# A decoder layer on eight cores: V tiles with a ones column, chained first loads, w_out sums on VectorE, and a merged last down projection

## The chip, the cores and the metric

The kernel runs on all 8 cores of one Trainium2 chip. Each core computes the whole layer for its own 1,152 tokens (1,024 of a prompt, 128 of samples), plus a small halo; the cores exchange nothing. The time is in device microseconds of the slowest core, lower is better.

In the profiled run of the kernel before, the clock record of cores 4 and 5 has 0.81 from 52 to 210 us, apart from shorter stretches at 0.50. So I read stage times from **quiet cores** (those whose clock was not lowered).

## The reference, cut to what matters

```python
h = rmsnorm(x); q, k, v, B, C, u = split(h @ w_in)
A = windowed attention(q, k, v)         # 16 heads, 4 KV heads, window 128, ALiBi, a sink logit in the denominator
S = B * dwconv3(C * u)                  # gated short convolution
x = x + concat(rmsnorm(A), rmsnorm(S)) @ w_out
h = rmsnorm(x)
x = x + (silu(dwconv3(h @ w_gate) + b) * (h @ w_up)) @ w_down     # d_model 2048, d_ff 5632
y = rmsnorm(x)
```

Softmax here needs two products with the same exponentials: their product with V, and their sum (the denominator).

## The kernel before

Activations lie feature-major: features on the 128 partitions, tokens along the free dimension. The stages are, in order: **stage one** (load x in three token tiles, and K, V, Q projections); **attention**, whose small matmuls are interleaved step by step with the dense B, C, u projections so that PE always has work; a **handover** that computes the two norm factors of the mixed halves; **w_out**; the **FFN** in 11 groups of gate, up and down; and the **end** (the last down projection, final norm, output). Matmuls are written through one helper (line L209 in the profile), most additions through another (L234), activations through L230, and so on; one profile line is therefore many places.

Stage one, the loads and the projections (cut):

```python
T.dma("sp", cf, cf_d)
xload(0)                                   # four DMAs, one per quarter of the features
wload(0)                                   # K weights; float32 in HBM, cast to bf16 by the DMA
T.dma("pool", cb, cb_d)
wload(1, after=[st0[0][:, 0, :]])          # "after": wait until that piece has landed
T.dma("sp", scT..., sct_d)
xload(1)
wload(2, after=[st0[0][:, 0, :]])
wload(3, after=[st0[0][:, 0, :]])
norm1(0)                                   # hT = x * g on VectorE, squares on ScalarE, their sums on VectorE
xload(2)
p = [k_task(0, 0), k_task(1, 0)]           # matmuls; the returned functions evict with the norm factor
rstd1(0, 7)                                # the norm factor, by a ones matmul and Ln/Exp
for f in p: f()
norm1(1)
for i in range(4): v_task(i)()
# ... tiles 1 and 2 in the same manner
```

Attention, the product with V (per block of 128 queries; `lt` holds exponentials, which are the stationary operand):

```python
oo = psb[b0 + half][:, g * 65:g * 65 + 64]
od = psb[b0 + half][:, g * 65 + 64:g * 65 + 65]
T.mm(oo, lt, vtm[:, vt, j * 64:(j + 1) * 64], start=(op == 0), stop=(op == 1), skip=True)
T.mm(od, lt, onesb[:, 0:1], start=False, stop=(op == 1), skip=True)       # the denominator: one column
```

The interleaving gives each dense step an equal share of the attention steps, though dense steps are 260, 384 or 512 columns wide:

```python
tgt = min(m, ((i + 1) * m + n - 3) // max(1, n - 2))
while si < tgt:
    step(pr, seq[si]); si += 1
```

Handover and w_out (48 steps, of 16 matmuls each: the attention half into pA, the convolution half into pB):

```python
rA_calc()
for ti in range(3): rB_calc(ti, 7)         # each with a reciprocal on VectorE
for oc in range(16):
    for ti, (a, b) in enumerate(FT):
        # 8 matmuls into pA, 8 into pB
        T.tt("dve", u1, pA[:, 0:W], rA[:, a:b], ALU.mult)
        T.tt("pool", x2, x2, u1, ALU.add)
        T.tt("dve", u2, pB[:, 0:W], accB[:, a:b], ALU.mult)
        T.tt("dve", x2, x2, u2, ALU.add)
        T.act(h2T[:, oc, a:b], x2, AF.Copy, scale=col(V_GF + oc))
        T.act(sq, x2, AF.Square)
        T.tt("pool", acc2[:, a:b], acc2[:, a:b], sq, ALU.add)
```

In the first gate/up step all three norm sums of the FFN (`r2_calc`) stand between the gate and the up matmuls. The end:

```python
LT = [(0, 512), (512, 1024), (1024, 1152)]
for ti, (a, b) in enumerate(LT):
    for oc in range(16):
        # 4 matmuls (group 10 alone)
        T.tt("dve", x3, ps[:, 0:W], x3, ALU.add)
        T.act(sq3[it % 2][:, 0:W], x3, AF.Square)
        T.tt("pool", acc3[:, a:b], acc3[:, a:b], sq3[it % 2][:, 0:W], ALU.add)
        # after oc 2: the norm of the tile before; then one output per step, scaled on VectorE
```

The softmax here doesn't subtract the row's maximum and nothing guards it: scores larger than these inputs give would overflow.

Of the kernel before, what the change touches and what calls it, by code (L numbers as in the profile page):

```python
# [8 lines left out]
ALU = mybir.AluOpType  # L9
# [294 lines left out]
FT = [(0, 385), (385, 770), (770, 1154)]  # L304
WINS = 18

def build_nc(same_engine_sync=True):
    nc = bass.Bass("TRN2", target_bir_lowering=False)  # L308
    with ExitStack() as es:
# [99 lines left out]
        vtm = V(o, [11, 256], BF16); o += 5632  # L409
# [3 lines left out]
        kf = V(o, [2, 256]); o += 2048  # L413
        vf = V(o, [2, 256]); o += 2048
# [20 lines left out]
        o = O_H2 + 36928  # L435
        rA = V(o, [NC]); o += 4616
# [42 lines left out]
        def xload(t):  # L479
            for q in range(4):  # L480
                T.dma("sp", st0[t][:, 4 * q:4 * q + 4, :], xt_d[t][:, 4 * q:4 * q + 4, :])
# [15 lines left out]
        def rstd1(t, bank):  # L497
            a, b = TX[t]
            W = b - a
            T.mm(psb[bank][:, 0:W], onesf, S4[t][:, 0, :])  # L500
            ln = S4[t][:, 1, :]
            T.act(ln, psb[bank][:, 0:W], AF.Ln, bias=epsc, scale=1.0 / D)
            T.act(r1[:, a:b], ln, AF.Exp, scale=-0.5)
            q0 = max(a, 126)
            T.act(r1q[:, q0 - 126:b - 126], ln[:, q0 - a:], AF.Exp, scale=-1.0)
            tl = [i for i, (c0, c1) in enumerate(VT) if a <= c0 < b]
            for i in tl:
                c0, c1 = VT[i]
                T.mm(psb[bank][0:c1 - c0, i:i + 1], r1[0:1, c0:c1], onesf[0:1, 0:1])
                T.copy("act", r1c[0:c1 - c0, i:i + 1], psb[bank][0:c1 - c0, i:i + 1])  # L510
# [4 lines left out]
        T.dma("pool", cb, cb_d)  # L515
        wload(1, after=[st0[0][:, 0, :]])
        T.dma("sp", scT.rearrange("p a b -> p (a b)"), sct_d)
        xload(1)
        wload(2, after=[st0[0][:, 0, :]])
        wload(3, after=[st0[0][:, 0, :]])  # L520
        norm1(0)
        xload(2)

        dbank = {"i": 0}

        def nb():
            b = dbank["i"] % 4
            dbank["i"] += 1
            return b
# [13 lines left out]
        def v_task(i):  # L543
            c0, c1 = VT[i]
            rows = c1 - c0
            ps = psb[nb()]
            for k in range(16):
                T.mm(ps[0:rows, 0:256], hT[:, k, c0:c1], wk(1, k, 0, 256), start=(k == 0), stop=(k == 15))

            def post():  # L550
                T.act(vtm[0:rows, i, :], ps[0:rows, 0:256], AF.Copy, scale=r1c[0:rows, i:i + 1])
                if i >= 9:
                    T.act(vf[:, i - 9, :], ps[:, 0:256], AF.Copy, scale=r1c[:, i:i + 1])
            return post
# [11 lines left out]

        p = [k_task(0, 0), k_task(1, 0)]
        rstd1(0, 7)
        for f in p:
            f()  # L570
        norm1(1)
        for i in range(4):
            v_task(i)()
        p = [q_task(0, 0, 2), q_task(1, 0, 2)]
        for f in p:
            f()
        k_p = [k_task(0, 1), k_task(1, 1)]
        rstd1(1, 6)
        for f in k_p:
            f()  # L580
        norm1(2)
        for i in range(4, 7):
            v_task(i)()
        for qc in range(2):
            q_task(qc, 1, 2)()
        for t in range(2):
            for qc in (2, 3):
                q_task(qc, t, 3)()
        k_p = [k_task(0, 2), k_task(1, 2)]
        wload(4)  # L590
        rstd1(2, 5)
        for f in k_p:
            f()
        T.dma("sp", kw_d, kf.rearrange("p a b -> p (a b)"))
        for i in range(7, 11):
            v_task(i)()
        wload(5)
# [6 lines left out]
        wload(7)  # L604

# [51 lines left out]
        def att_PV(pr, G, bl):  # L657
            n = 2 * G + bl + 1
            b0 = ab2()
            for g in range(4):  # L660
                for half in range(2):
                    j = 2 * pr + half
                    for op in range(2):
                        oo = psb[b0 + half][:, g * 65:g * 65 + 64]
                        od = psb[b0 + half][:, g * 65 + 64:g * 65 + 65]
                        lt = Ef_(half, g)[:, (op * 2 + bl) * 128:(op * 2 + bl + 1) * 128]
                        vt = n + 1 - op
                        T.mm(oo, lt, vtm[:, vt, j * 64:(j + 1) * 64], start=(op == 0), stop=(op == 1), skip=True)
                        T.mm(od, lt, onesb[:, 0:1], start=False, stop=(op == 1), skip=True)
# [40 lines left out]
        def halo_PV(pr):  # L710
            b0 = ab2()
            for g in range(4):
                for half in range(2):
                    j = 2 * pr + half
                    s = slice(half * 8 + g * 2, half * 8 + g * 2 + 2)
                    oo = psb[b0 + half][0:2, g * 65:g * 65 + 64]
                    od = psb[b0 + half][0:2, g * 65 + 64:g * 65 + 65]
                    T.mm(oo, EhO[:, s], vtm[:, 1, j * 64:(j + 1) * 64], start=True, stop=False, skip=True)
                    T.mm(od, EhO[:, s], onesb[:, 0:1], start=False, stop=False, skip=True)
                    T.mm(oo, EhP[0:2, s], vtm[0:2, 0, j * 64:(j + 1) * 64], start=False, stop=True, skip=True)  # L720
                    T.mm(od, EhP[0:2, s], onesb[0:2, 0:1], start=False, stop=True, skip=True)
# [49 lines left out]
        def samp_PV(pr):  # L771
            b0 = ab2()
            X, Y = psb[b0], psb[b0 + 1]
            for half in range(2):
# [4 lines left out]
                T.mm(X[pb:pb + 64, :], vtm[:, 10, j * 64:(j + 1) * 64], en, start=True, stop=False, skip=True)  # L779
# [89 lines left out]
        def att_seq(pr):  # L869
# [14 lines left out]
            out += [("SS", 0), ("SS", 1), None, ("SP",)]  # L884
# [30 lines left out]
        def run(pr, dense):  # L915
# [4 lines left out]
            for i, d in enumerate(dense):  # L920
# [9 lines left out]
                tgt = min(m, ((i + 1) * m + n - 3) // max(1, n - 2))  # L930
# [6 lines left out]
                late.clear()  # L937
            while si < m or early or late or trq:
# [41 lines left out]
        run(1, bdense(range(4, 8)))  # L980
        T.dma("sp", cvo_d, cuk.rearrange("p a b -> p (a b)"))

# [7 lines left out]
        def rB_calc(ti, bank):  # L990
            a, b = FT[ti]
# [3 lines left out]
            T.recip(ln[:, 0:W], r1q[:, a + 2:b + 2])  # L995
            T.ts("dve", ln, ln, EPS, None, ALU.mult)
            T.stt("dve", ln, psb[bank][:, 0:W], 1.0 / 1024, ln, ALU.mult, ALU.add)
            T.act(ln, ln, AF.Ln)
            T.act(accB[:, a:b], ln, AF.Exp, scale=-0.5)

        def rA_calc():
# [6 lines left out]
            b0 = 4  # L1008
            dg = Af[0]
            T.tt("dve", dg[0:2, 0:2], ident[0:2, 0:2], rAc[0:2, 0:1].to_broadcast([2, 2]), ALU.mult)  # L1010
            T.mm(psb[6][:, 0:2], onesf[0:2, :], dg[0:2, 0:2])
# [5 lines left out]
            dgs = [V(O_H2 + 8192 + 4752 + 2048 + 2176 + i * 512, [128]) for i in range(8)]  # L1017
            for n in range(1, 9):
                T.ts("dve", dgs[n - 1], ident, rAc[:, n:n + 1], None, ALU.mult)
# [5 lines left out]
        rA_calc()  # L1025
        for ti in range(3):
            rB_calc(ti, 7)

        it = 0
        for oc in range(16):  # L1030
            si = WINS + oc // 2
            T.dma("sp", x2T[:, oc, :], xr_d[oc])
            for ti, (a, b) in enumerate(FT):
                W = b - a
                pA, pB = psb[(2 * it) % 8], psb[(2 * it + 1) % 8]
                for k in range(8):
                    T.mm(pA[:, 0:W], wk(si, k, oc % 2), mixedT[:, k, a:b], start=(k == 0), stop=(k == 7))
                for k in range(8, 16):
                    T.mm(pB[:, 0:W], wk(si, k, oc % 2), mixedT[:, k, a:b], start=(k == 8), stop=(k == 15))
# [3 lines left out]
                T.tt("pool", x2, x2, u1, ALU.add)  # L1043
# [9 lines left out]
            if oc % 2 == 1:  # L1053
                wload(si + 4)
# [38 lines left out]
        calc = {"todo": True}  # L1093

        def gateup(grp):
            ab = actb[grp % 2]
            for hg in range(2):
# [3 lines left out]
                for ci in range(2):  # L1101
                    f = grp * 4 + hg * 2 + ci
                    fi = hg * 2 + ci
                    for ti, (a, b) in enumerate(FT):
# [7 lines left out]
                        if calc["todo"]:  # L1112
                            for t_ in range(3):
                                r2_calc(t_, 4 + t_)
                            calc["todo"] = False
# [52 lines left out]
        for grp in range(11):  # L1168
            gateup(grp)
            if grp >= 1:  # L1170
# [5 lines left out]
        ab = actb[0]  # L1176
        LT = [(0, 512), (512, 1024), (1024, 1152)]
        acc3 = V(O_H2, [1152])
        r3 = V(O_H2 + 4608, [1152])
        sq3 = [V(O_H2 + 9216 + i * 2048, [512]) for i in range(2)]  # L1180
        yst = V(O_H2 + 9216 + 4096, [4, 512])

        def fin_calc(ti):
            a, b = LT[ti]
            W = b - a
            bank = ti
            T.mm(psb[bank][:, 0:W], onesf, acc3[:, a:b])
            ln = sq3[0][:, 0:W]
# [3 lines left out]
        def fin_out(ti, oc):  # L1192
            a, b = LT[ti]
            x3 = x2T[:, oc, 2 + a:2 + b]
            T.stt("dve", x3, x3, col(V_GN + oc), r3[:, a:b], ALU.mult, ALU.mult)
            T.dma("sp", yt_d[oc, :, a:b], x3)

        pend = []
        it = 0
        for ti, (a, b) in enumerate(LT):  # L1200
            W = b - a
            for oc in range(16):
                ps = psb[4 + it % 4]
                for fi in range(4):
                    T.mm(ps[:, 0:W], dview(d0 + fi // 2)[:, fi % 2, oc * 128:(oc + 1) * 128], ab[:, fi, a:b],
                         start=(fi == 0), stop=(fi == 3))
                x3 = x2T[:, oc, 2 + a:2 + b]
                T.tt("dve", x3, ps[:, 0:W], x3, ALU.add)
                if oc == 0:
                    T.act(acc3[:, a:b], x3, AF.Square)  # L1210
                else:
                    T.act(sq3[it % 2][:, 0:W], x3, AF.Square)
                    T.tt("pool", acc3[:, a:b], acc3[:, a:b], sq3[it % 2][:, 0:W], ALU.add)
                it += 1
                if oc == 2 and ti > 0:
                    fin_calc(ti - 1)
                    pend += [(ti - 1, x) for x in range(16)]
                if pend:
                    fin_out(*pend.pop(0))
            
        for q in pend:
            fin_out(*q)
        fin_calc(2)
# [165 lines left out]
```

## Time and profile before

Three executions took 1704.71, 1738.67 and 1952.89 us. The profiled one took 1704.54. The list of cores of the kernel before (span and mean granted clock):

```profile
...
core 0: 1683.7 us, clock 0.974
...
core 4: 1702.6 us, clock 0.954
core 5: 1703.5 us, clock 0.954
...
core 7: 1685.1 us, clock 0.972
```

Six cores end at 1682 to 1685 us. Cores 4 and 5 had their clock lowered early and end about 20 us later.

Next the chain of waits, summed by engine, from the page of the slowest core (core 5):

```profile
...
PE 74%; POOL 7%; DVE 7%; issue 5%; ACT 4%; DMA 3%; SPq 0%; DVEq 0%; POOLq 0%; ACTq 0%
```

PE bounds most of it, but not all. Where the rest lies, the table by windows of quiet core 0 tells. I set the windows at the stage borders found in the trace: stage one, attention with the handover, w_out, the first gate matmul to the first up matmul, FFN, end. Columns are the window and its length, busy microseconds of each engine with the number of instructions, granted clock, mean share of busy DMA engines, and GB/s.

```profile
...
core 0: us, PE busy (x) PEld busy (x) DVE busy (x) ACT busy (x) POOL busy (x), PEclk, DMA share, GB/s
0.00:133.00 133.00, 86.33 (x493) 53.25 (x494) 49.76 (x84) 32.18 (x46) 4.76 (x12) 0.92 0.61 143
133.00:418.00 285.00, 272.91 (x2428) 166.93 (x2427) 159.69 (x399) 111.93 (x291) 60.96 (x81) 0.98 0.42 78
418.00:580.00 162.00, 133.03 (x770) 72.84 (x769) 70.24 (x137) 45.94 (x90) 79.71 (x91) 0.99 0.36 83
580.00:597.00 17.00, 7.77 (x22) 3.10 (x23) 5.90 (x12) 6.65 (x14) 9.42 (x12) 0.68 1.22 224
597.00:1571.00 974.00, 971.30 (x5938) 577.93 (x5937) 610.42 (x1177) 97.59 (x264) 148.78 (x196) 1.00 0.42 69
1571.00:1683.00 112.00, 74.22 (x391) 37.44 (x388) 83.18 (x146) 30.34 (x58) 47.76 (x47) 0.84 0.32 101
```

The FFN has PE busy for 971 of 974 us: nothing to gain there. Time without PE work lies in stage one (47 us), around the handover (12), in w_out (29), before the first up matmul (9) and in the end (38). The waits of PE on the same core (total, times, longest) name who was waited for:

```profile
...
PE psb L209 <- DVE arena L234: 49.9, 64, 3.6
PE psb L209 <- ACT arena L230: 20.7, 6, 8.8
PE psb L209 <- POOL arena L234: 18.8, 6, 7.0
PE psb L209 <- DMA arena<-win: 17.9, 1, 17.9
```

The 29.0 us of w_out are among the 49.9 us put down to VectorE. But one must ask what VectorE itself waited for, and the chain of waits, in order of time, tells it (start, duration, engine). These lines are one step of w_out on core 0, and the start of the next:

```profile
...
442.75 0.57 DVE arena L234
...
443.40 1.04 ACT arena L230 x2
...
444.51 1.83 POOL arena L234 x2
...
446.37 0.57 DVE arena L234
```

In each step, the two POOL additions take 1.83 us, ScalarE 1.04 and one VectorE addition 0.57, one after the other. The step takes 446.37 − 442.75 = 3.62 us, of which PE needs only 2.61 (16 matmuls that start 163 ns apart). POOL is in the loop, so it binds. The handover and the end show up in the same chain, as a reciprocal of 2.58 us (there are three) and as POOL additions without a break:

```profile
...
412.83 2.58 DVE arena L268
...
1614.35 1.28 POOL arena L234
...
1615.70 1.29 POOL arena L234
```

Last, two groups of the list by shape (busy time, mean ns of one | idle before): the products with V and with the ones column.

```profile
...
L209 PE MATMUL psb<-arena 128*128 128x64 bf16 x256 | 16.5, 190 | 2.1 <-DVE arena L234 2.0
L209 PE MATMUL psb<-arena 128*128 128x1 bf16 x256 | 16.0, 165 | 0.0
```

### The profile page before, as it was taken

To read this page: it belongs to the slowest core of one execution; us is meant where nothing else is said; L and a number is where in the kernel's file an instruction comes from. 1 tells how busy PE (TensorE), PEld (TensorE's weight loads), DVE (VectorE), ACT (ScalarE), POOL (GpSimd) and SP (SyncE) were. 2 spreads that over 40 slices of the span, in tenths; PEclk is the share of its full clock that TensorE was granted. 3 is DMA by queue.
4 is the path that set the end of the run, shared out by engine and by line. 5 is a ranking of instruction groups with operands and counts; after the bars stand their busy time and mean duration, and the time that the engine had idled before them with its cause. 6 is when DMAs were issued, how large, how long until landed. Compare 5 with 4: busy or idle time off the path is not lost.

```text
span 1703.5 us, 24149 instructions; the slowest of 8 cores (1681.7 to 1703.5 us)
## 1 busy us (share of the span) xinstructions
PE 1567.0 (92%) x10034; PEld 918.0 (54%) x10034; DVE 979.5 (58%) x1953; ACT 325.9 (19%) x761; POOL 351.4 (21%) x438
## 2 busy tenths in 40 slices
PE   2789999998887779999999999999999999999973
PEld 1555565655444345555555555555555556555531
DVE  3523563555543445575665757575656657575767
ACT  2312341444222221101001010101011010101042
POOL 0001121122255432111111010101111120101064
PEclk8778899999899989999999999999999999999985
DMA  9516236223922293533533534434435335335205
GB/s 197 169 31 118 50 51 99 50 51 67 256 43 45 44 171 60 87 62 53 92 54 62 87 50 74 75 50 76 73 50 82 68 50 94 55 61 88 44 34 189
DMA packets 26414, 136.98 MB, mean 80 GB/s; under 512 B 3072, under 2 KB 5376, under 8 KB 13952
## 3 DMA queue, kind: packets, MB, share of 16 engines
q0 software_dynamic: 13968, 98.92, 35.5%
q1 hardware_dynamic: 12336, 36.52, 7.2%
q8 instruction: 78, 1.28, 0.3%
q14 instruction: 32, 0.26, 0.1%
HBM read 223.47 MB, written 14.80 MB: 140 GB/s over the span
## 4 chain that ended last, share of the span: by engine, by line
PE 74%; POOL 7%; DVE 7%; issue 5%; ACT 4%; DMA 3%; SPq 0%; DVEq 0%; POOLq 0%; ACTq 0%
PE psb L209 74%; POOL arena L234 7%; ACT arena L230 4%; DVE arena L234 4%; DMA arena<-xt 3%; DVE arena L253 2%; DVE arena L246 0%; DVE arena L268 0%; PE psb L213 0%; POOL arena L204 0%; SPq L204 0%; ACT L230 0%; ACT arena L258 0%; DVE arena L260 0%; DVEq L169 0%
## 5 line engine op out<-in xcount | busy, mean ns | idle before, releaser
L209 PE MATMUL psb<-arena 128*128 128x384 bf16 (+8 forms) x9962 | 1564.4, 318 | 124.6 <-DVE arena L234 48.4
L209 PEld LDWEIGHTS psb<-arena 128*128 128x128 bf16 (+2 forms) x9962 | 912.9, 100 | 769.9 <-issue 66.8
L234 DVE TENSOR_TENSOR arena<-psb,arena 128x384 f32<-128x384 f32 (+10 forms) x1172 | 569.5, 504 | 506.3 <-POOL arena L234 226.2
L234 POOL TENSOR_TENSOR arena<-arena 128x385 f32<-128x385 f32 (+8 forms) x316 | 293.9, 935 | 873.4 <-ACT arena L230 795.9
L230 ACT ACTIVATE arena<-arena 128x385 f32<-128x385 f32 (+15 forms) x402 | 232.7, 601 | 1223.1 <-DVE arena L253 896.6
L253 DVE SCALAR_TENSOR_TENSOR arena<-arena 128x383 f32<-128x383 f32 (+3 forms) x360 | 231.2, 646 | 24.9 <-ACT arena L230 13.9
L234 DVE TENSOR_TENSOR arena<-arena 128x512 bf16<-128x512 bf16 (+9 forms) x149 | 82.6, 564 | 135.2 <-POOL arena L234 95.0
L246 DVE TENSOR_SCALAR arena<-arena 128x385 f32<-128x385 f32 (+9 forms) x215 | 88.6, 429 | 43.4 <-DMA arena<-xt 30.7
L230 ACT ACTIVATE arena<-psb,arena 128x256 bf16<-128x256 f32 (+5 forms) x167 | 64.6, 474 | 93.0 <-PE psb L209 92.8
L204 POOL DMA_DIRECT2D arena<-wu x22 | 12.4, 565 | 263.1 <-PE psb L209 263.1
L204 POOL DMA_DIRECT2D arena<-win x18 | 10.3, 574 | 169.3 <-PE psb L209 158.1
L258 ACT COPY arena<-arena 128x2 f32<-128x2 f32 (+1 forms) x140 | 23.8, 200 | 0.0
L258 ACT COPY arena<-psb 128x512 bf16<-128x512 bf16 (+5 forms) x31 | 12.0, 395 | 48.3 <-PE psb L213 43.7
L268 DVE RECIPROCAL arena<-arena 128x4 f32<-128x4 f32 (+3 forms) x39 | 14.0, 360 | 3.5 <-ACT arena L230 2.3
L204 POOL DMA_DIRECT2D arena<-wd x22 | 12.3, 562 | 0.2
L260 POOL COPY arena<-arena 128x2 f32<-128x2 f32 (+5 forms) x20 | 5.1, 269 | 32.7 <-DVE arena L234 31.6
L204 POOL DMA_DIRECT2D arena<-wg x22 | 11.8, 538 | 0.0
L213 PEld LDWEIGHTS psb<-arena 128*128 128x128 bf16 (+1 forms) x72 | 5.2, 99 | 3.5 <-issue 1.9
L213 PE MATMUL psb<-arena 128*128 128x128 bf16 (+1 forms) x72 | 6.5, 217 | 0.0
L253 DVE SCALAR_TENSOR_TENSOR arena<-psb,arena 128x8 f32<-128x8 f32 (+4 forms) x15 | 5.2, 374 | 0.7 <-PE psb L209 0.3
L204 POOL DMA_DIRECT2D arena<-wout x8 | 4.6, 574 | 0.3 <-issue 0.3
L230 ACT ACT_TABLE_LOAD x3 | 3.8, 1283 | 2.1 <-PEq L308 1.1
(11 smaller groups left out, 7.6 us busy)
## 6 DMA issues: line engine op xcount, KB each, us to landing
arena<-wg POOLq DMA_DIRECT2D x22, 1024.0 KB, 16.1
arena<-wu POOLq DMA_DIRECT2D x22, 1024.0 KB, 10.3
arena<-wd POOLq DMA_DIRECT2D x22, 1024.0 KB, 14.5
arena<-win POOLq DMA_DIRECT2D x18, 1024.0 KB, 10.8
arena<-xr SPq DMA_DIRECT2D x16, 577.0 KB, 21.8
arena<-wout POOLq DMA_DIRECT2D x8, 1024.0 KB, 10.0
yt<-arena SPq DMA_DIRECT2D x32, 256.0 KB, 2.1
arena<-xt SPq DMA_DIRECT2D x4, 1024.0 KB, 14.5
```

Source lines behind the costliest of these rows:

```text
L204: return self.add(q, lambda: eo.dma_start(out=out, in_=in_), [in_, *after], [out], dma=q)
L209: return self.add("pe", lambda: nc.tensor.matmul(out, lhsT, rhs, start=start, stop=stop, **kw), [lhsT, rhs], [out])
L213: return self.add("pe", lambda: nc.tensor.transpose(out, in_, ident), [in_, ident], [out])
L230: return self.add("act", lambda: nc.scalar.activation(out=out, in_=in_, func=func, **kw), rd, wr)
L234: return self.add(eng, lambda: eo.tensor_tensor(out=out, in0=in0, in1=in1, op=op), [in0, in1], [out])
L246: return self.add(eng, lambda: eo.tensor_scalar(out=out, in0=in0, scalar1=s1, scalar2=s2, op0=op0, **kw), rd, [out])
L253: return self.add(eng, lambda: eo.scalar_tensor_tensor(out=out, in0=in0, scalar=scalar, in1=in1, op0=op0, op1=op1), rd, [out])
L258: return self.add("act", lambda: nc.scalar.copy(out=out, in_=in_), [in_], [out])
L260: return self.add(eng, lambda: eo.tensor_copy(out=out, in_=in_), [in_], [out])
L268: return self.add("dve", lambda: nc.vector.reciprocal(out=out, in_=in_), [in_], [out])
```

## The change

Intent, part by part: (1) V tiles get a ones column, so that one 65-column matmul gives both product and denominator. (2) The first loads are chained, so that they arrive one after the other in the order of use instead of all at once; stage one's tasks are reordered and may use 8 PSUM banks, and its copies of the norm factors into columns are made one per token tile. (3) The norm factors of the handover are computed inside the last dense steps of attention, without reciprocals, and w_out starts with the convolution half. (4) In w_out one of POOL's two additions goes to VectorE. (5) The three norm sums of the FFN are spread over three steps. (6) Groups 9 and 10 of w_down are merged into one pass over token tiles of 512, 384 and 256, with sums on VectorE and outputs on VectorE, ScalarE and POOL.

The diff, cut to its core (cuts marked `# ...`). Some names: `xq(t, q)` is the first piece of quarter q of token tile t of x, so `after=[xq(0, 2)]` waits for its landing; `nb()` gives the next PSUM bank and `flush(p)` runs evictions; attention runs in two halves of 36 dense steps, and `keep` is how many dense steps at the end of a half get no new attention steps (2 before; 5 now in the second half), and `hook` holds the functions that are called in them and compute the norm factors of the handover. I call their matmuls and waits "the hook".

```diff
-        vtm = V(o, [11, 256], BF16); o += 5632
+        vtm = V(o, [11, 260], BF16); o += 5720
# ...
         T.dma("sp", cf, cf_d)
         xload(0)
         wload(0)
-        T.dma("pool", cb, cb_d)
-        wload(1, after=[st0[0][:, 0, :]])
-        T.dma("sp", scT.rearrange("p a b -> p (a b)"), sct_d)
-        xload(1)
-        wload(2, after=[st0[0][:, 0, :]])
-        wload(3, after=[st0[0][:, 0, :]])
+        wload(1, after=[xq(0, 2)])
+        wload(2, after=[xq(0, 3)])
+        xload(1, after=[wslot[1][:, 0:1]])
+        wload(3, after=[xq(1, 1)])
+        T.memset("dve", vtm.rearrange("p i (j d) -> p i j d", j=4)[:, :, :, 64:65], 1.0)
         norm1(0)
-        xload(2)
# ... xload(2) now after xq(1, 3), cb after xq(2, 0); the order of the stage-one tasks:
         p = [k_task(0, 0), k_task(1, 0)]
-        rstd1(0, 7)
-        for f in p:
-            f()
-        norm1(1)
-        for i in range(4):
-            v_task(i)()
-        p = [q_task(0, 0, 2), q_task(1, 0, 2)]
+        p += [v_task(i) for i in range(4)]
+        rstd1(0, nb())
+        flush(p)
+        p = [q_task(0, 0, 2), q_task(1, 0, 2)]
+        flush(p)
+        norm1(1)
# ... tiles 1 and 2 likewise
-                        oo = psb[b0 + half][:, g * 65:g * 65 + 64]
-                        od = psb[b0 + half][:, g * 65 + 64:g * 65 + 65]
+                        oo = psb[b0 + half][:, g * 65:g * 65 + 65]
-                        T.mm(oo, lt, vtm[:, vt, j * 64:(j + 1) * 64], start=(op == 0), stop=(op == 1), skip=True)
-                        T.mm(od, lt, onesb[:, 0:1], start=False, stop=(op == 1), skip=True)
+                        T.mm(oo, lt, vtm[:, vt, j * 65:(j + 1) * 65], start=(op == 0), stop=(op == 1), skip=True)
# ...
-                tgt = min(m, ((i + 1) * m + n - 3) // max(1, n - 2))
+                tgt = min(m, ((i + 1) * m + n - keep - 1) // max(1, n - keep))
# ...
+                if hook and si == m and not early and not trq:
+                    hook.pop(0)(i - n)
# ... rB_calc: the reciprocal and two VectorE operations replaced by one multiplication
-        rA_calc()
-        for ti in range(3):
-            rB_calc(ti, 7)
+        def hookB(left):
+            rA_calc()
+            rB_calc(0, 6)
+            rB_calc(1, 7)
+        run(1, bdense(range(4, 8)), keep=5, hook=[lambda left: rA_pre(), hookB])
# ... w_out:
+            if oc == 0:
+                pre = [wo_mm(0, t, 8) for t in range(3)]
+                rB_calc(2, nb())
# ...
-                T.tt("pool", x2, x2, u1, ALU.add)
+                T.tt("dve", x2, x2, u1, ALU.add)
# ... gate/up:
-                        if calc["todo"]:
-                            for t_ in range(3):
-                                r2_calc(t_, 4 + t_)
-                            calc["todo"] = False
+                        if it < 3:
+                            r2_calc(it, 4 + it)
# ... end:
-            if grp >= 1:
+            if 1 <= grp < 10:
                 down(grp - 1)
-        LT = [(0, 512), (512, 1024), (1024, 1152)]
+        LT = [(0, 512), (512, 896), (896, 1152)]
# ... per step: 8 matmuls over groups 9 and 10 (the first eight oc do f 0..5 ahead), then
                 T.tt("dve", x3, ps[:, 0:W], x3, ALU.add)
+                if accp:
+                    T.tt(*accp.pop())
# ...
-                    T.tt("pool", acc3[:, a:b], acc3[:, a:b], sq3[it % 2][:, 0:W], ALU.add)
+                    if ti < 2 or oc < 15:
+                        accp.append(("dve" if ti < 2 else "pool", acc3[:, a:b], acc3[:, a:b], sq3[oc % 2][:, 0:W], ALU.add))
+                    else:
+                        last = sq3[oc % 2][:, 0:W]
```

## The prediction

> **What bounds it now.** By the list of cores, six cores end at 1682–1685 us and cores 4 and 5 at 1703; the slowest sets the time. The chain of waits is 74% PE, so the matmuls bound most of the kernel. The table by windows shows the FFN middle (640–1590 us) at 99–100% busy PE and clock 1.00. By stage (core 5, timeline and chain):
> - 0–58 us: PE waits for loads. The chain holds 44.6 us of DMA of x; two x tiles and four weight tiles share the engines. The stage's last projection ends at about 129 us on undisturbed core 0.
> - Attention to about 420 us: PE 100% busy.
> - 420–436 us: PE almost idle (reciprocals of 2.55 us, small chains), then cold: matmuls start 320 ns apart instead of 163. [...]
> - w_out, 436–606 us: one step per 3.68 us, of which PE needs 16 x 163 ns = 2.61. The chain alternates POOL (two adds, 1.7–1.95 us), DVE and ACT: POOL binds.
> - 606–616 us: PE idle behind three r2 sums that wait for POOL.
> - 1594–1703 us: down group 9 is dense; then POOL adds of 1.28–1.33 us per step bind; then a serial tail.
>
> **What changes, and its worth (estimates from the durations above).**
> 1. Ones column: 256 one-column matmuls of 64 ns (16.3 us busy) and 32 halo ones of about 83 ns vanish; 64 columns become 65, about free. PE is critical there: −18 us.
> 2. Chained loads: x0 and w0 come alone (about 17 us from the queues' busy shares), x2 at about 62 us. PE holds 67 us of warm matmuls in this stage, so it can't end before the x2 work: about 97 instead of 129 us: −30 us.
> 3. Norm factors hooked into the last dense steps, reciprocals gone, conv half first: the 16 us hole and its re-warming go: −14 us.
> 4. w_out add to DVE: four DVE operations at about 0.58 us = 2.35 us < 2.61, POOL one at 0.9: PE binds. 48 x 1.05 = −49 us.
> 5. r2 sums spread over three steps: −8 us.
> 6. Merged end: PE 128 matmuls each of 512, 384 and 256 columns, 62 us. DVE adds, accumulates (0.69 + 0.69 us) and scales, finishing about 80 us after the last gate/up instead of 110: −27 us; DVE, not PE, binds the last part.
>
> Sum −146 us. Undisturbed cores: about 1540. Cores 4 and 5 ran at clock 0.81 until about 210 us and lost 20 us; denser early work loses slightly more: **1563 us** in a fast run, 8-in-10 range 1535–1605 (the slow state is the upper part). Faster by over 2%: 0.97; within 2%: 0.02; slower: 0.01.
>
> **What would show it.**
> - First slices: PE past its stage-one work near 97 us (116 on cores 4/5).
> - No 128x1 matmul group; POOL's share of the chain near nothing.
> - w_out steps near 2.65 us, 127–132 us in all. If steps stay above 2.9, DVE binds instead.
> - No PE gap over 4 us between attention and gate/up.
> - The FFN middle unchanged, 94.4 us per group.
> - Last matmul 65–72 us after the last gate/up, tail 10–18 us, with DVE.
>
> **What would make it wrong.** x2T loads cannot begin before attention releases the memory; they could starve the first w_out steps. Chaining may leave DMA idle between links. [...] The slow state, seen in two of three runs before, adds 2% or more.

18 + 30 + 14 + 49 + 8 + 27 = 146 us, which leaves about 1540 of the 1683 us of a quiet core. The 23 us on top are the 20 us that cores 4 and 5 lost in the trace and 3 of the author's estimate for denser early work. "Cold" and "warm" stand for a granted clock of 0.50 and of 1.00: on core 5 of the kernel before the clock record has 0.50 from 431.5 to 441.8 us, and w_out's matmuls start 321 ns apart there and 163 ns after it. That this slow stretch goes with the hole ("re-warming") was an estimate. Of the risks named last, idle DMA between links did show: on core 0 of the changed kernel the mean DMA share was 0.09 from 22 to 23 us and 0.00 from 23 to 24.

## More of the kernel before

Most executions of one kernel agree closely, but not all. In some, one or two pairs of neighbouring cores show a lower granted TensorE clock in the mean (0.952 to 0.958 in the kernel before, where the other cores have 0.966 to 0.976) and end about 20 us later.

In other runs the four cores of one half of the chip show a mean clock of 0.80 to 0.95.

## The result, and the profile after

The changed kernel took 1594.3 us (median of four, 1593.66 to 1594.93), and it was correct. The kernel before took 1721.69 us (median of four: the three named above and 1686.83, run beside it). The ratio of fast runs is 0.9417, with a 95% interval of 0.9347 to 0.9488. A ratio is the mean time of one kernel's fast runs over that of the other's of the same rounds, so it is not quite the ratio of the medians. The fast runs of the kernel before are one with a lowered pair and one without; against the latter alone, 1686.83 us, the ratio would be 0.945.

The list of cores of the changed kernel:

```profile
...
core 0: 1592.6 us, clock 0.983
...
core 2: 1583.8 us, clock 0.988
...
core 5: 1589.4 us, clock 0.987
```

No core was lowered, in any of the four runs. So the fair comparison is quiet core with quiet core: their mean went from 1683.2 us (six cores) to 1588.5 us (eight), a gain of 94.7 us. The prediction expected 146 us for a quiet core. The table splits both by stage. Stage borders come from the trace: the first 260-column B/C/u matmul, the first 385-column w_out matmul, the first up matmul (so that the wait for r2 counts to w_out), and the last gate/up matmul.

| Stage, mean of quiet cores | before | after | measured | predicted |
|---|---|---|---|---|
| stage one | 132.6 | 114.4 | −18.2 | −30 |
| attention and handover | 284.6 | 275.5 | −9.1 | −18 − 14 = −32 |
| w_out and the wait for r2 | 178.8 | 130.7 | −48.1 | −49 − 8 = −57 |
| FFN | 973.9 | 974.0 | +0.2 | 0 |
| end | 113.2 | 93.9 | −19.4 | −27 |
| sum (terms rounded) | 1683.2 | 1588.5 | −94.7 | −146 |

The chain of waits by engine, from the page of the changed kernel (core 0):

```profile
...
PE 81%; DVE 6%; DMA 5%; issue 4%; ACT 3%; POOL 2%; SPq 0%; DVEq 0%; POOLq 0%; ACTq 0%
```

PE's share rose from 74 to 81%, POOL's fell from 7 to 2%. The table by windows of core 0, again with the stages as windows and the same columns:

```profile
...
0.00:115.00 115.00, 83.94 (x491) 49.78 (x492) 49.22 (x85) 30.68 (x39) 4.62 (x12) 0.93 0.74 165
115.00:391.00 276.00, 266.35 (x2140) 160.82 (x2139) 154.32 (x395) 110.82 (x289) 58.98 (x79) 0.99 0.35 63
391.00:518.00 127.00, 126.24 (x770) 74.64 (x768) 111.17 (x194) 51.06 (x98) 45.23 (x52) 1.00 0.62 146
518.00:521.00 3.00, 3.00 (x19) 1.87 (x18) 1.29 (x3) 1.03 (x2) 1.24 (x2) 1.00 0.15 30
521.00:1496.00 975.00, 971.71 (x5943) 578.22 (x5942) 610.09 (x1178) 104.93 (x272) 150.93 (x199) 1.00 0.42 72
1496.00:1592.00 96.00, 70.51 (x393) 40.66 (x390) 65.41 (x115) 37.04 (x71) 31.28 (x29) 0.85 0.36 118
```

In w_out PE is now busy for 126 of 127 us, and POOL's busy time there fell from 79.7 to 45.2 us; VectorE rose from 70.2 to 111.2 and still fits. In stage one PE's own work is nearly the same (86.3 before, 83.9 now), so almost the whole gain was waiting. The waits of PE on core 0:

```profile
...
PE psb L209 <- DMA arena<-win: 19.6, 2, 18.2
PE psb L209 <- DVE arena L234: 14.7, 19, 4.8
PE psb L209 <- DVE arena L246: 7.5, 5, 2.1
PE psb L209 <- ACT arena L230: 5.6, 4, 1.7
PE psb L209 <- DMA arena<-wd: 2.7, 1, 2.7
```

The wait for the first weights, 17.9 us before, has not moved (the longest is 18.2). Waits for VectorE's L234 fell from 49.9 to 14.7 us. The chain of waits shows what remained and what is new: at the start; in attention; in w_out, one unbroken piece; and in the end:

```profile
...
2.43 19.00 DMA arena<-xt
21.98 11.17 DMA arena<-win
...
143.70 4.16 ACT arena L230 x10
...
404.44 111.26 PE psb L209 x680
...
1497.62 11.41 DMA arena<-wd
...
1541.72 0.74 DVE arena L253
1542.46 1.08 DVE arena L234 x2
...
1543.93 0.74 DVE arena L253
1544.67 1.08 DVE arena L234 x2
```

The line at 143.70 is ten exponentials of attention on which PE waits. Lines at 1541.72 and after are a VectorE chain of 2.21 us per step (0.74 + 1.08 + 0.39 of issue), where PE's 8 matmuls of 384 columns need 8 x 163 = 1.30 us. And the list by shape has one group in place of two:

```profile
...
L209 PE MATMUL psb<-arena 128*128 128x65 bf16 x256 | 11.8, 194 | 3.2 <-DVE arena L234 3.1
```

By this page busy time fell by 16.5 + 16.0 − 11.8 = 20.7 us, but the stage did not get that much shorter. That was the first thing to explain.

### The profile page after: what moved, and what is told of

The parts are those of the page before. It is cut to its first block, busy times and chain, and to the rows that moved or that the text cites. A ratio compares the mean times of both kernels' runs of the same rounds, so it can differ in the third digit from the quotient of the medians.

```text
span 1592.6 us, 23451 instructions; the slowest of 8 cores (1583.8 to 1592.6 us)
## 1 busy us (share of the span) xinstructions
PE 1521.8 (96%) x9748; PEld 906.0 (57%) x9748; DVE 991.5 (62%) x1968; ACT 335.6 (21%) x771; POOL 292.3 (18%) x372
## 4 chain that ended last, share of the span: by engine, by line
PE 81%; DVE 6%; DMA 5%; issue 4%; ACT 3%; POOL 2%; SPq 0%; DVEq 0%; POOLq 0%; ACTq 0%
PE psb L209 80%; DVE arena L234 3%; ACT arena L230 3%; DMA arena<-wu 2%; DVE arena L253 2%; POOL arena L234 2%; DMA arena<-xt 1%; DMA arena<-wd 1%; DVE arena L246 1%; DMA arena<-win 1%; PE psb L213 0%; ACT L230 0%; ACT arena L258 0%; SPq L204 0%; POOL arena L204 0%
## 5 line engine op out<-in xcount | busy, mean ns | idle before, releaser
L209 PE MATMUL psb<-arena 128*128 128x384 bf16 (+11 forms) x9676 | 1519.1, 319 | 54.0 <-DMA arena<-win 19.6
L209 PEld LDWEIGHTS psb<-arena 128*128 128x128 bf16 (+3 forms) x9676 | 901.3, 99 | 665.3 <-issue 21.7
L234 DVE TENSOR_TENSOR arena<-psb,arena 128x384 f32<-128x384 f32 (+10 forms) x1127 | 547.8, 502 | 501.8 <-POOL arena L234 227.5
L230 ACT ACTIVATE arena<-arena 128x385 f32<-128x385 f32 (+15 forms) x415 | 239.1, 601 | 1119.8 <-DVE arena L253 870.4
L234 POOL TENSOR_TENSOR arena<-arena 128x385 f32<-128x385 f32 (+7 forms) x250 | 234.6, 939 | 847.8 <-ACT arena L230 793.4
L253 DVE SCALAR_TENSOR_TENSOR arena<-arena 128x383 f32<-128x383 f32 (+4 forms) x347 | 218.3, 633 | 11.0
L234 DVE TENSOR_TENSOR arena<-arena 128x512 bf16<-128x512 bf16 (+10 forms) x230 | 141.6, 621 | 45.5 <-ACT arena L230 39.9
L246 DVE TENSOR_SCALAR arena<-arena 128x383 f32<-128x383 f32 (+9 forms) x212 | 88.1, 434 | 25.9 <-DMA arena<-xt 15.4
L230 ACT ACTIVATE arena<-psb,arena 128x256 bf16<-128x256 f32 (+6 forms) x167 | 64.3, 475 | 84.5 <-PE psb L209 84.4
L258 ACT COPY arena<-psb 128x512 bf16<-128x512 bf16 (+6 forms) x24 | 10.9, 460 | 36.8 <-PE psb L213 34.6
```

Of the source, the lines that this page charges most:

```text
L209: return self.add("pe", lambda: nc.tensor.matmul(out, lhsT, rhs, start=start, stop=stop, **kw), [lhsT, rhs], [out])
L230: return self.add("act", lambda: nc.scalar.activation(out=out, in_=in_, func=func, **kw), rd, wr)
L234: return self.add(eng, lambda: eo.tensor_tensor(out=out, in0=in0, in1=in1, op=op), [in0, in1], [out])
L246: return self.add(eng, lambda: eo.tensor_scalar(out=out, in0=in0, scalar1=s1, scalar2=s2, op0=op0, **kw), rd, [out])
L253: return self.add(eng, lambda: eo.scalar_tensor_tensor(out=out, in0=in0, scalar=scalar, in1=in1, op0=op0, op1=op1), rd, [out])
L258: return self.add("act", lambda: nc.scalar.copy(out=out, in_=in_), [in_], [out])
```

## The experiments

Twelve kernels ran, all with correct results, on four chips. The two theories to be told apart, for every part of the gap, were: (A) the removed work or wait cost less on the critical path than it was booked at; (B) it was worth what was booked, but the changed kernel gives it back in new waits. Where a kernel is named "before with ...", the kernel before is edited; "changed with ..." edits the changed kernel. The kernel before was run beside each set. The changed kernel was not run again, so comparisons with it can cross chips; the kernel before, in fast runs without a lowered pair, took 1686.0 to 1689.3 us on all four.

### Before with the ones column alone (`b_ones`)

The edit is part 1 of the change: the wider V tile, the memset and the 65-column matmul, as in the diff above.

> Kernel before with the ones column alone. Theory A (the prediction): each one-column matmul cost 64 ns of PE, so the stretch from the first to the last B/C/u matmul on an undisturbed core shrinks from 266 us to about 248 and the kernel by 18 us. Rival B: the true price is the 35 ns between the starts of matmuls (10 us in all), 65 columns cost 41 ns where 64 cost 29 (3 to 4 us back), and what PE no longer does it then waits for ACT and DVE: the stretch stays at 260 to 267 us and the kernel gains 0 to 6 us.

Measured: 1701.23 us median; ratio 0.9994 (0.9891 to 1.0097). That says nothing by itself, since on this chip both kernels ran now with a lowered pair and now without one (before: 1686.35 to 1686.73 or 1704.43 to 1706.42); a fourth run of this one was slow, 1768.2. Quiet run against quiet runs it is 1682.2 against 1686.6, that is −4.4. Attention with handover took 281.2 us on its six quiet cores (280.3 to 282.0) where the kernel before took 284.6 (283.5 to 285.0): **−3.4 us, not −18**, within the rival's 0 to 6.

### Before with the one-column matmuls doubled (`b_ones_twice`)

```diff
                         T.mm(od, lt, onesb[:, 0:1], start=False, stop=(op == 1), skip=True)
+                        T.mm(psb[b0 + half][:, 260 + g:261 + g], lt, onesb[:, 0:1], start=False, stop=(op == 1), skip=True)
```

The extra sums go to an unused PSUM column. This measures the disputed cost in place.

> Kernel before with every one-column matmul of the 16 prompt blocks done twice, the second into an unused PSUM column (256 more; results unchanged). Theory A: 64 ns each, +16 us. Rival B: 35 ns each, +9 us or less, as part of it is hidden in waits that PE had anyway.

Measured: the profile fell on an execution with cores 4 to 7 lowered, so I read its four undisturbed cores 0 to 3: attention 290.1 to 290.7 us, +5.9 us against 284.6 for 256 more matmuls, or **23 ns each**. (Run times: 1691.66 us in the one quiet run, 1711 to 1904 in the others; ratio 1.0033, 0.9903 to 1.0163.) At 64 ns each it would have been 16 us. The start times in the trace agree: in the kernel before, a one-column matmul starts 28 ns after its 64-column partner and the next one starts 26 ns after it (medians), a pair every 54 ns; in the changed kernel 65-column matmuls start 30 ns apart. So the column saves 24 ns x 256 = 6.1 us of PE time (6.9, if the 32 one-column matmuls of the halo, which also go, cost the same). The rival had the right sign and the wrong price: it put 35 ns on each. In the kernel with the doubled ones, the second starts 27 ns after the first. The mean duration of 165 ns is about six times these distances, so most of it, and of the busy union of 16.0 us, is time in which other matmuls run too.

### Changed without the ones column (`a_no_ones`)

The wide tiles stay, the pairs of matmuls come back.

```diff
-                        T.mm(oo, lt, vtm[:, vt, j * 65:(j + 1) * 65], start=(op == 0), stop=(op == 1), skip=True)
+                        T.mm(oo, lt, vtm[:, vt, j * 65:j * 65 + 64], start=(op == 0), stop=(op == 1), skip=True)
+                        T.mm(od, lt, onesb[:, 0:1], start=False, stop=(op == 1), skip=True)
```

> Changed kernel with the value and denominator matmuls split again (V tiles keep their layout). Theory A: +18 us, about 1612. Rival B: within 5 us of the 1594 of the changed kernel, with PE's waits before the value matmuls (8 waits of 0.3 to 0.9 us on core 0) smaller or gone.

Measured: fast runs 1593.42 and 1594.06 us, as the changed kernel's (1593.66 to 1594.93); two more, 1624.55 and 1625.06, had lowered pairs; ratio 0.9398. Attention with handover 275.8 us on seven cores (278.8 on the eighth) against 275.5 on all eight. **In the changed kernel the column is worth 0.3 us.** And since attention without it still went from 284.6 to 275.8, the other edits there (the hook, no reciprocals, the repacking that came with `keep=5`) are worth about 9 us of the 14 booked. Both theories hold a part: 6.1 of 18 us is what PE time the column can save, and most of that 6.1 was given back. The trace of core 0 says where. Before the hook the profile's waits of PE are 6.6 us in sum with the column and 4.6 without it; six of the ten over 0.25 us come before 65-column matmuls, which wait for exponentials and masks. The 384-column matmuls there start 167 ns apart instead of 163 on the average, 1.8 us over 448 of them; that is ten of them which start 320 ns apart. The record of the granted clock has the reason: two stretches of 3.4 us at clock 0.50 (core 0 of the changed kernel, columns as in the tables by windows).

```profile
...
215.70:219.10 3.40, 3.40 (x12) 1.62 (x11) 1.71 (x6) 1.66 (x5) 0.00 (x0) 0.50 0.02 5
376.10:379.50 3.40, 3.40 (x18) 3.31 (x17) 0.15 (x1) 1.79 (x6) 1.00 (x1) 0.50 0.00 0
```

The first holds those ten matmuls. The second lies in the hook, which takes 7.9 us with the column (the wait and the float32 matmuls after it) and 6.2 without. All eight cores of the changed kernel have both stretches; seven cores of `a_no_ones` have none in attention, and the eighth, the one with 278.8 us, has one of 6.8 us in the hook. So 2.0 + 1.8 + 1.7 = 5.5 us are found of the 5.8 that were given back. This is read from the traces and no edit forced it.

### Changed with attention paced by width (`a_pace`)

If ScalarE's exponentials are late because narrow dense steps get as many attention steps as wide ones, then giving each dense step a share by its columns should remove waits.

```diff
-                tgt = min(m, ((i + 1) * m + n - keep - 1) // max(1, n - keep))
+                wd = [(260, 384, 512)[(q // 3) % 3] for q in range(n)]
+                tgt = min(m, -(-sum(wd[:i + 1]) * m // sum(wd[:n - keep])))
```

> Changed kernel with the attention steps spread over the dense steps by their width (260, 384, 512 columns) and not by their count, so that fewer of them fall in the short steps. If the ones column's gain was turned into waits for ACT's exponentials and DVE's masks in the short steps (rival B), the attention stretch of core 0 (275.6 us with the hook's 8) shrinks by 5 to 12 us. If PE's own work bounds the stretch, it stays within 2 us.

Measured: attention with handover 269.3 to 269.4 us on all eight cores, **−6.1 us**, as theory B had it; of these 1.7 lie in the hook, where the half-clock stretch is missing, and 4.4 before it. The means of the other stages moved by at most 1.1 us; fast runs 1587.5 to 1591.27 us, one with a lowered pair at 1612.73; ratio 0.9363 (its kernel before had runs with a lowered pair, which flatters it).

### The same without the ones column (`a_pace_no_ones`)

> The paced attention of the earlier run, but with the value and denominator matmuls split again. Theory (the ones column saves some 6 us of PE work, which the unpaced changed kernel gives back as waits for ACT and DVE): with those waits thinned out by the pacing the split costs 3 to 6 us, the attention stretch is 272 to 276 us against 269.4. If the ones column is worth nothing in any case, the stretch stays at 269 to 271.

The edit joins the last two. Measured: 272.3 us on six cores, 275.3 on two; 1591.22 us median (1590.25 to 1594.02), ratio 0.9431. With the pacing, the column is worth 2.9 us, at the lower end of the 3 to 6 expected. Like must be compared with like here: the same attention code takes 3 us longer on cores whose trace has a further stretch of 6.8 us at clock 0.50 in the hook (these two, and three cores of `a_combo2` below, which has the column, with 272.5). Shorter with shorter is 272.3 against 269.4, longer with longer 275.3 against 272.5. So the small saving is real, and how much of it is kept depends on how the steps are packed.

### Before with w_out's addition on VectorE alone (`b_wout_dve`)

```diff
-                T.tt("pool", x2, x2, u1, ALU.add)
+                T.tt("dve", x2, x2, u1, ALU.add)
```

> Kernel before with one add of the output projection moved from POOL to DVE and nothing else. Theory: POOL's two adds set the pace and the r2 wait behind it is mostly POOL's backlog, so one cause was booked twice in the prediction (49 + 8 us). Output projection plus first gate up to first up matmul: 179 us before; with this edit alone 136 to 142 (the projection at 127 to 131, the r2 wait falls from 14.5 to 6 to 10 us without being touched). If the r2 wait is a cost of its own, it stays at 14 us.

Measured: 1640.49 us median (1639.55 to 1641.11), where the kernel before took 1688.18 on the chip; ratio 0.972 (0.9703 to 0.9736). In the profile w_out went from 162 to 126.6–127.7 us, with PE never idle there. The table by windows of its core 0 says it in one line:

```profile
...
418.00:545.00 127.00, 127.00 (x772) 75.31 (x770) 111.22 (x194) 49.51 (x96) 44.27 (x51) 0.99 0.53 119
```

And the stretch from the first gate to the first up matmul fell from 17.1 to 4.6 us, though the r2 sums were left as they were. Together the two stretches fell by 46.9 us to 131.9 (136 to 142 were expected), of the 48.1 that the whole change gains there. **One line of the change is half of its gain.** The r2 wait was the tail of POOL's backlog, which the faster w_out no longer leaves; the prediction booked it a second time. In the changed kernel, where the sums are spread as well, it is 3.3.

### Changed with x1 ahead of the Q weights (`a_x1_first`)

Is the rest of stage one a matter of the order of loads? PE works out of tile 0 and then waits for tile 1; here x1 is loaded before w2.

```diff
         wload(1, after=[xq(0, 2)])
-        wload(2, after=[xq(0, 3)])
-        xload(1, after=[wslot[1][:, 0:1]])
-        wload(3, after=[xq(1, 1)])
+        xload(1, after=[xq(0, 3)])
+        wload(2, after=[xq(1, 1)])
+        wload(3, after=[xq(1, 3)])
```

and tile 1's K and V tasks ahead of tile 0's Q tasks.

> Changed kernel; the loads in another order: x1 asked for when x0 has landed (no longer after w1), w2 only after half of x1, w3 and x2 after all of x1, and the projections of x1's K and V before any Q. Theory: stage one of the changed kernel (about 114 us to the first B/C/u matmul, 82 of them forecast as 65 us of DMA plus the x2 work) is late because w1 and w2 share the DMA engines and x1 waits for w1 and stands behind w2; then x1 lands near 38 us instead of 48 and the stage ends at 100 to 105 us, the kernel gains 8 to 13 us. Rival: the DMA engines are full from 5 to 70 us in any order, x2 cannot land before about 68 us, and all Q of t=0 and t=1 still has to wait for w2 and w3: the stage stays at 110 to 116 us.

Measured: stage one 115.8 to 121.3 us, no shorter than 112.8 to 116.4; fast runs 1593.26 to 1596.32 us (one slow, 1816.13); ratio 0.9452. On core 0 x1's last piece landed at 44.1 us instead of 49.5, yet the timeline shows VectorE starting its normalisation at 45.65 (47.28 in the changed kernel), behind the evictions of K, and waiting for ScalarE inside it. So earlier data did not help, and the order of loads as the cause was a miss. It is not a clean test, as the edit also takes tile 0's Q tasks out of the gap that they filled. That the chain of squares, sums and scaling sets the pace is a guess at this point.

### Changed with the normalisation split, two attempts (`a_norm`, `a_norm2`)

Now that chain itself. In the changed kernel VectorE scales four features, then waits for ScalarE's squares to add them, and so on; PE waits for the scaled features. The first attempt scaled all 16 features first and had ScalarE square x in place:

```diff
+        def norm_h(t):                     # all 16 scalings, nothing else
+            for k in range(16):
+                T.ts("dve", hT[:, k, a:b], x[:, k, :], col(V_GA + k), None, ALU.mult)
+        def norm_s(t):                     # squares and sums, later
+            for q in range(4):
+                T.act(x[:, 4 * q:4 * q + 4, :], x[:, 4 * q:4 * q + 4, :], AF.Square)
+                # ... sums into x[:, 0:4, :] on VectorE
```

> Changed kernel, loads in its own order. The scaling of x to h is cut off from the sums of squares: all 16 scalings of x1 and x2 come first on DVE, the squares are written in place (no shared buffer that makes ACT and DVE take turns), and the norm factor of x0 is taken before V. Theory after the failed reordering: not the landing of x1 (44 to 48 us) but the chain behind it on DVE and ACT holds PE (h of x1 is complete only at 56 us, its V and norm factor at 67 us, PE is dense only from 67.5 us on); then stage one ends at 98 to 105 us instead of 113 to 117 and the kernel gains 9 to 15 us. Rival: loads bind; then the stage stays within 4 us.

Measured: stage one **125.5 to 128 us, slower**; fast runs 1604.57 and 1605.57 us, three more slow (1745 to 1894); ratio 0.9517. The fault is in the edit: the chained weight loads wait for a piece of x by *reading* it, so overwriting x in place must wait until those loads have gone. The waits of ScalarE on its core 2, from 15 to 50 us:

```profile
...
ACT arena L230 <- DMA arena<-win: 17.0, 2, 10.0
```

17 us of waiting for weight DMAs, which it needs for nothing. In both attempts the tasks move too: tile 0's norm factor is taken before V, and tile 1's Q matmuls come before its norm factor. The second attempt keeps the split and writes the squares to spare buffers:

```diff
-                T.act(x[:, 4 * q:4 * q + 4, :], x[:, 4 * q:4 * q + 4, :], AF.Square)
+                T.act(sqbuf(t, q), x[:, 4 * q:4 * q + 4, :], AF.Square)
```

> The same cut of the first norms without its fault: squares written in place had to wait for the weight loads that are chained on the same tile (ACT waited 17 us for DMA of w_in on core 2). The squares now go to buffers of their own. Theory as before (the chain on DVE and ACT behind x1 holds PE): stage one ends at 98 to 106 us. Rival (loads bind): 112 to 117.

Measured: stage one 108.3 to 111.9 us, mean 109.7, **−4.7**; fast runs 1587.43 to 1589.36 us, one slow (1795); ratio 0.9419 (0.9399 to 0.9439) against 1686.07. That lies between the two expectations (98 to 106, or 112 to 117): the chain holds part of the stage, not all of what was hoped. How much of the 4.7 comes from the moved tasks was not tested. The timelines of VectorE for tile 1 show the mechanism, first of the changed kernel, then of this one:

```profile
...
47.28 2.72 DVE L246 TENSOR_SCALAR arena<-arena 128x384 bf16<-128x384 f32 x8
...
51.58 1.40 DVE L246 TENSOR_SCALAR arena<-arena 128x384 bf16<-128x384 f32 x4
...
54.94 1.40 DVE L246 TENSOR_SCALAR arena<-arena 128x384 bf16<-128x384 f32 x4
```

```profile
...
44.36 5.35 DVE L246 TENSOR_SCALAR arena<-arena 128x384 bf16<-128x384 f32 x16
```

The 16 scalings ran in three pieces until 56.3 us, waiting for squares in between; now they are one piece, done at 49.7. What still stands in stage one is the first wait for weights (18.0 us on core 0) and waits of 7.8 us in sum, where the changed kernel has 12.8.

### Changed with the final sums on PE (`a_end_pe`)

The end's middle third is bound by VectorE (2.21 us per step). Here squares are written in bf16, and PE sums them with a ones matmul into a PSUM bank. Not shown: seven banks rotate instead of eight, and half of the second tile's outputs go from VectorE to ScalarE and POOL:

```diff
-                    T.act(sq3[oc % 2][:, 0:W], x3, AF.Square)
-                    # ... accumulated on VectorE or POOL
+                T.act(sqb[(ti * 16 + oc) % 4][:, 0:W], x3, AF.Square)
+            T.mm(QB[:, 0:b - a], onesw, sqb[(ti * 16 + oc) % 4][:, 0:b - a], start=(oc == 0), stop=(oc == 15), skip=True)
```

> Changed kernel with the last norm's sums taken off DVE: squares written in bf16 and summed by PE with a matmul by ones (48 more matmuls, about 8 us of PE), seven banks in rotation instead of eight. Theory: DVE binds the merged end (2.21 us per step in the middle third where PE needs 1.30); without its 32 adds of 0.55 to 0.69 us PE binds again, the end shrinks from about 94 us to 83 to 88. Rival: the end is bound by PE and the output tail; then it gets longer by up to 8 us.

Measured: the end takes 87.2 to 91.1 us, mean 89.4 against 93.9, **−4.5** (83 to 88 us were expected); fast runs 1588.32 to 1590.42 us, two slow (1750, 1880); ratio 0.9417 (0.9394 to 0.944). PE's waits for VectorE and POOL in the end (4.8 and 2.3 us on core 2) are gone, as the theory of a VectorE bound has it: the sums and the moved outputs both come off VectorE, and which of them counts more was not tested. But one wait grew: for the last down weights, from 1.2 to 3.5 us. This is its line, and it is now PE's longest wait in the end:

```profile
...
PE psb L209 <- DMA arena<-wd: 3.5, 1, 3.5
```

### Everything that helped, together (`a_combo`, `a_combo2`)

The first joined pacing, sums on PE and the flawed normalisation; the second has the mended one.

> Changed kernel with this cut of the first norms, the attention steps paced by width and the last norm's sums on PE. If the three act in different stages their gains add: 10 to 14 us in stage one, 6 in attention, 4 to 5 at the end, so 1564 to 1574 in a fast run (0.92 to 0.93 of before).

> Changed kernel with the mended cut of the first norms, the paced attention and the last norm's sums on PE. If the gains add: 1564 to 1574 in a fast run; if stage one does not move: 1576 to 1582.

Measured: the first 1596.69 us (1595.15 to 1597.37, ratio 0.9464), with stage one at 123 to 128 us eating the gains of attention (269.3 to 272.6) and the end (86 to 91). The second **1579.96 us (1579.77 to 1580.11), ratio 0.937 (0.9355 to 0.9384)**: stage one 109 to 112, attention 269.3 to 272.6, end 86.5 to 91. It is about 14 us faster than the changed kernel. The expectation was missed: 1564 to 1574 assumed 10 us or more in stage one, and the three gains measured one by one (4.7 + 6.1 + 4.5 = 15.3 us) nearly add: the mean of the eight cores fell from 1588.5 to 1574.5.

## Why the prediction was right or wrong

The direction, and most mechanisms, were right: the FFN did not move (974 us), w_out became PE-bound at 127.4 us (predicted 127 to 132), no PE gap over 4 us is left between attention and gate/up, and POOL's share of the chain fell from 7% to 2%. The gain was mis-sized: for a quiet core 146 us were predicted and 94.7 measured, a miss of 51 us. The time on record, 1563 us, missed by only 31, and that is luck: 23 us for a lowered pair of cores were added that none of the four runs showed, while the slowest of the eight cores ends about 4 us after their mean. The steps that failed, as the prediction put them:

1. **"256 one-column matmuls of 64 ns (16.3 us busy) ... vanish; 64 columns become 65, about free ... −18 us."** This is the clearest error of reading. The trace's start times give 24 ns saved per pair, the doubled kernel 23 ns: 6.1 us (6.9 with the halo) at most, 3.4 in the kernel before, 0.3 in the changed one as it stands. The busy time of this group was not what went when the group went: it was 16.0 us, and 6.1 are saved. The start-to-start distance had the right price: 26 ns after a one-column matmul, where the prediction booked 64.
2. **"Norm factors hooked into the last dense steps ... −14 us."** About 9 us measured, which is what attention gained without the column (`a_no_ones`). The mechanism was right. On core 0 the hole of 18.8 us (399.14 to 417.96) became 6.2 us there: a wait of 2.7 and 3.5 of float32 matmuls that PE must still do. But the rest of attention took 269.5 us there instead of 266.2, so 3.3 of the 12.6 us went back. Of these 2.5 lie before the second half (from 148.6 to 151.1 us), where `keep` is as it was, so making room for the hook explains little of it; the cause is open. I did not isolate the hook in a run of its own.
3. **"It can't end before the x2 work: about 97 instead of 129 us: −30 us."** Measured 132.6 to 114.4. PE's own work in the stage is 84 us, of which about 10 is the price of matmuls at half clock (386-column matmuls start about 320 ns apart then; the sum of such excess distances on core 0); with the first wait of 18 us, for which the chaining could do nothing since x0 and w0 were first in line before too, that is 102 us already. The estimate counted 67 us of matmuls at full clock and left room for neither. The remaining 12 us were further waits, of which the run with the split normalisation took 4.7. Nor did x2 come at "about 62 us": its last piece landed at 71.4 us on core 0 (66.1 in the kernel before). That did not bind, since PE had other work from 67 us on and waited only 2.7 us more in this stage. As for the half clock, the record of core 0 of the changed kernel has five stretches at 0.50 in the first 380 us: 6.8 us each from 24.5 and from 51.8 us (mean clocks of 0.73 from 20 to 30 us and of 0.66 from 50 to 60), and 3.4 us each from 68.9, 215.7 and 376.1. The longest waits of PE just before each, or across its start, were 2.1, 1.7, 1.2, 1.7 and 2.7 us, the first wait of 18.2 us left aside. But a wait of 1.4 us that ended at 100.4 us was followed by no such stretch, so what brings one on was not shown.
4. **"w_out add to DVE: ... −49 us" and "r2 sums ... −8 us".** Measured 48.1 us for both, 46.9 for the first alone. Two symptoms of one backlog were booked as two gains.
5. **"Merged end ... finishing about 80 us after the last gate/up instead of 110: −27 us; DVE, not PE, binds the last part."** Measured −19.4: the last matmul came 76 to 81 us after the last gate/up where 65 to 72 was expected, then a tail of 13.5 to 17 us. That VectorE binds was right, and the kernel with sums on PE bears it out with −4.5. Not foreseen were the wait for the down weights (2.7 us on core 0) and float32 ones matmuls that wait for VectorE and POOL (4.8 and 2.5 us).
6. **"Cores 4 and 5 ran at clock 0.81 ... denser early work loses slightly more."** Taken as a part of the kernel, it was a state of the execution: in the kernel before some runs show it (1704 us) and some don't (1686), and the four runs of the changed kernel do not. In the profiled run of the kernel before, cores 4 and 5 have a mean clock of 0.80 and 0.79 from 80 to 205 us, where core 0 has 0.97. And denser work did not lower the clock in the profiled run of the changed kernel: on all eight cores it was 1.00 from 382 to 1500 us, which holds w_out and the 974 us of the FFN. This error of +23 us hid half of the others. Two runs of the changed kernel without its column, and one of the paced one, show that such pairs do not vanish with the change (1613 to 1625 us).

In sum, over the first five: 18 + 14 − 9.1 = 23 us in attention, 12 in stage one, 9 in w_out and r2, 8 in the end. They have one form in common. Each stage was costed as if it became as dense as its busiest engine, and no stage but w_out did.

Open remain: the hook and the repacking in attention as runs of their own; what the moved tasks and the split are worth apart in stage one; whether the first 18 us could be shortened (smaller first pieces of the weights were not tried); and whether the half-clock stretches can be avoided, of which each of 3.4 us cost about 1.7 in attention.

## What to carry to other kernels

Price a matmul that you mean to remove by the start-to-start distance of its neighbours, or double it in place and see; its busy time or mean duration contains others' time (64 and 165 ns here, for a saving of 24). When one slow engine is in a loop, count everything that stands behind its backlog once: moving one addition brought 46.9 us here, including the wait after the stage. And when a stage is to become dense, add up its first wait, the time lost to a lower clock and its own work (18, about 10 and 74 us here in stage one) before claiming a new end time; then look for the serial chain (here scale, square, add) that earlier data did not shorten here.
